# Output projection of a two-layer encoder by seven quadrant products, with weights summed by adding DMAs

## The chip, the cores and the metric

One core of a Trainium2 chip runs the whole program. The metric is device time per execution in microseconds (us); the median of repeated executions stands for a kernel.

The core has engines that run side by side, each with an in-order queue: PE (TensorE, matmuls), DVE (VectorE), ACT (ScalarE), POOL (GpSimd) and SP (SyncE, which here only issues DMAs). They wait for each other by semaphores. SBUF is the on-chip memory, PSUM the banks that matmuls write to.

## The reference

Two layers, 512 tokens, 1024 channels, all in float32. What matters here:

```python
def _mixer_sublayer(...):
    ...
    gates = jax.nn.sigmoid(gl + b_gate)
    ga, gb = jnp.split(gates, N_BRANCHES, axis=-1)
    return jnp.einsum('bsd,de->bse', ga * ya + gb * yb, w_out)

def reference(...):
    for i in range(DEPTH):
        h = _mixer_sublayer(...)
        x = _layer_norm(DEEPNORM_ALPHA * x + h, ln1_g[i], ln1_b[i])
        mlp = square(relu(x @ w_up[i])) @ w_down[i]
        gate = sigmoid(x @ w_ple_gate[i] + b_ple_gate[i])
        ple = gate * (p[i] @ w_ple[i])
        x = _layer_norm(DEEPNORM_ALPHA * x + mlp + ple, ln2_g[i], ln2_b[i])
```

`ya` and `yb` are the outputs of two kinds of attention, each with a projection of its own; `w_out` is the output projection that the change concerns, 512 x 1024 by 1024 x 1024 in each layer.

## The kernel before

**Products.** A float32 product is made of three matmuls: each operand is split into a high part, rounded to PE's format, and a low part, the rest; hi·hi, hi·lo and lo·hi are added in PSUM (`mm3`, `mm3t`). One matmul has 128 rows of depth and 512 columns of output.

**Weights.** They lie packed in DRAM (`wst`) in the order of use. `fetch` (L274) loads 128x1024 of them (512 KB) by SP into one of a few slots named `wst`; `prep` splits them. `split` (L248) takes the high part on ACT (a cast) and the low part on DVE (source minus high). `split_later` (L253) takes both on ACT, the low one as minus the high part, and POOL then issues an *adding DMA* that adds the source to it; which weights go that way is in the list `LATER`. High and low parts are tiles `whi`/`wlo` (three of each) or, for weights that stay longer, `bhi`/`blo`. A load is issued a few blocks ahead of use (`LOOK`), as soon as its slot is free.

**Order in a layer.** Attention; then for u = 0..3 the *second gates*: two gates (2u and 2u+1, of 128 channels each) as 24 matmuls each, tanh on ACT, then two `yb` products of 6 matmuls, a DVE step gate x `yb`, a POOL step that adds the first branch (`gate <- gate + ga`), and the split of the merged channels for the next product (`ahm` on ACT, `alm` on DVE). Then the output projection `wo`: 4 token tiles by 2 halves of 512 output channels by 8 depth blocks by 3 matmuls. DVE adds each result into the residual tile `y` (`projected`), takes its statistics (`moments`), and normalises (`normed`). PE transposes the normalised `y` (`turned`), and `embedding` (`ple`, from the input `p`, loaded as `pf` and split to `ph`/`pl`) and the embedding's gate (`embed`, `pg`) follow. Then comes the MLP, whose down projection already is made by seven products of quadrants in place of eight (class `Down`): both factors are cut into 2 x 2 blocks, seven products of sums of blocks are made, and each is added into or taken from one or more quadrants of the result. The weight sums are made on DVE there (`raw <- raw + raw`).

**What sets the order.** PE's order in these stages is that of the code (`manual_schedule`). A scheduler places the instructions of the other engines; within a queue each waits for those ahead of it. Pools (`np1`, `wb`, `rp`, ...) give tiles their memory, and a tile in memory that another used before waits for that one's last user.

Of the kernel before, what the change touches and what calls it, by code (L numbers as in the profile page):

```python
# [26 lines left out]
FQ = 4  # L27
UP_ORDER = (0, 4, 1, 5, 2, 6, 3, 7)
# [4 lines left out]
LATER = ((0, ("ple", 1, 0)), (1, ("start", 0)), *((l, n) for l in range(DEPTH) for n in (  # L33
# [27 lines left out]
def plan_layer(l):  # L61
# [31 lines left out]
    for u in range(4):  # L93
        out += [gate(1, 2 * u), gate(1, 2 * u + 1)]
        out.append((("bb", u), [("w_branch_b", l, [(i * P, P)], cols((t * P, P)))
                                for t in (2 * u, 2 * u + 1) for i in range(2)]))
# [5 lines left out]
    for h in range(2):  # L102
        out += k_outer(f"wo{h}", "w_out", blocks[4 * h:4 * h + 4])
# [17 lines left out]
def down_plan():  # L121

    return [((l, q, j, d, c), [("w_down", l, [((q * 8 + j * 4 + c * 2 + i) * P, P)], [(d * 512 + m * P, P)])
                               for i in range(2) for m in range(4)])
            for l in range(DEPTH) for q in range(FQ) for j in range(2) for d in range(2) for c in range(2)]
# [98 lines left out]
def build(nc, tc, plan, down, xw, xN, pT, wst, vec, rows, sink, cst, out):  # L224
# [3 lines left out]
    with ctx:  # L228
# [57 lines left out]
        def prep(c):  # L286
            st = fetched.pop(c)
            n = st.shape[-1]
            pool, tag, bufs = held_sets.get(plan[c][0][1][0], (wp, "w", 3))
# [37 lines left out]
        def linear(key, xs, ps=None):  # L327
            w = weights(key)
# [81 lines left out]
        def attention_block(l, av, rp, vt, OA, OB, begun):  # L410
            ct = rp.tile([P, cst.shape[1] - P], F32, tag="ct", name=f"ct{l}", bufs=1)
# [563 lines left out]
        def gate(l, b, t, vt, rp, ps=None):  # L975
            ps = linear((l, ("g", b, t)), X) if ps is None else ps
# [5 lines left out]
        class Tokens:  # L982


            def __init__(self, pool, y, name):
                self.pool, self.y, self.name, self.st, self.rs = pool, y, name, None, {}
# [19 lines left out]
            def steps(self, a, n=2, root=False, centre=True):  # L1006
# [8 lines left out]
                nc.vector.tensor_scalar(v, self.mv[:, a:a + n, 1], LN_EPS, None, ALU.add)  # L1015
# [71 lines left out]
        class Down:  # L1087
# [52 lines left out]
            def hidden(self, q, m, ps):  # L1140
# [16 lines left out]
                sr = self.qp.tile([P, 4, 256], F32, tag="sr", name=f"sr{self.l}_{q}_{kt}", bufs=1)  # L1157
# [14 lines left out]
            def half(self, q, n, s, c0=0, c1=512):  # L1172
# [3 lines left out]
                if first and not (s or c0):  # L1176
# [6 lines left out]
                for c in range(2):  # L1183
                    w = self.sets[n, c]
                    for i in range(2):
                        k, cols = 2 * c + i, slice(i * 512 + c0, i * 512 + c1)
                        for m, (a, b) in enumerate(((hi, 0), (hi, 1), (lo, 0))):
                            nc.tensor.matmul(ps, a[:, k, tok], w[b][:, cols], start=first and not (k or m),  # L1188
                                             stop=k == 3 and m == 2, skip_group_check=True)
# [16 lines left out]

        def pool(name, side="left"):
            c = ExitStack()
            return c.enter_context(tc.tile_pool(name=name, bufs=1, side=side, reuse_waits="tile")), c.close
# [6 lines left out]
        def embedding(l, h, PL, to, some=range(4)):  # L1216
            if 0 in some:
                ple["w"] = weights((0 if not h else l, ("ple", l, h)), 0)
            for a in some:
                ps = bank("mm", f"ple{l}_{h}_{a}")  # L1220
# [5 lines left out]
        for l in range(DEPTH):  # L1226
# [6 lines left out]
            oah, oal = (rp.tile([P, 4, S], F32R, name=f"oa{e}{l}", tag="oa" + e, bufs=1) for e in "hl")  # L1233
# [4 lines left out]
            ga = attention_block(l, av, rp, vt, OA, OB, begun)  # L1238
            av_close()

# [5 lines left out]
            np1, np1_close = pool(f"np{l}")  # L1246

            def pair(name):
                return (np1.tile([P, S], F32R, tag="ah", name="ah" + name, bufs=8),
                        np1.tile([P, S], F32R, tag="al", name="al" + name, bufs=8))  # L1250

            M = []
            for u in range(4):
                gs = [gate(l, 1, t, vt, np1) for t in (2 * u, 2 * u + 1)]
                w = weights((l, ("bb", u)))
                with in_turn(l):
                    nc.sync.dma_start(y[u], kept[u] if l else xN[u])
                if l and u:
                    add_row(y[u - 1], l - 1, 4)
                for n, g in enumerate(gs):  # L1260
                    t = 2 * u + n
# [8 lines left out]
                    M.append((mh, ml))  # L1270
            if l:
                add_row(y[3], l - 1, 4)
            rp_close()


            ph, pl = (np1.tile([P, 2, S], F32R, tag="p" + e, name=f"p{e}{l}", bufs=1) for e in "hl")
# [4 lines left out]
            split(ph, pl, pf)  # L1281
            PL = [(ph[:, k], pl[:, k]) for k in range(2)]
            wb, wb_close = pool(f"wb{l}", "right")
            held_sets.update({n: (wb, "b", 7) for n in ("wo1", "pg0", "pg1")})
            tn = Tokens(np1, y, f"n1_{l}")

            def projected(a, h, ps):
                x = y[a][:, h * 512:(h + 1) * 512]
                nc.vector.scalar_tensor_tensor(x, x, ALPHA, ps, ALU.mult, ALU.add)
                tn.moments(a, h)  # L1290
# [13 lines left out]
            def embed(a, h, ws):  # L1304
# [4 lines left out]
                t = np1.tile([P, S], F32, tag="tg", name=f"tg{l}_{h}_{a}", bufs=3)  # L1309
# [5 lines left out]
            with tc.manual_schedule(engines={PE}):  # L1315
                pss = [bank(t, f"wo{l}_0_{a}") for a, t in enumerate(("mm", "mm", "s", "s"))]
                for j in range(4):
                    w = weights((l, ("wo0", j)), 3)
                    for a in range(4):
                        for i in range(2):  # L1320
                            k = 2 * j + i
                            mm3t(pss[a], tokens(M[k], a), w, i, k == 0, k == KT - 1)
                for a in range(4):
                    projected(a, 0, pss[a])
                    if l:
                        ple[0, a] = np1.tile([P, S], F32, tag="ple0", name=f"ple{l}_0_{a}", bufs=4)
                        with in_turn(l):
                            nc.sync.dma_start(ple[0, a], kept_ple[a])
                ws = [weights((l, ("wo1", j)), 3 - j) for j in range(4)]
                for a in range(4):  # L1330
                    ahead(at[0] + a)
                    ps = bank("mm", f"wo{l}_1_{a}")
                    for k in range(KT):
                        mm3t(ps, tokens(M[k], a), ws[k // 2], k % 2, k == 0, k == KT - 1)
                    projected(a, 1, ps)
                    if a % 2:
                        normed(a - 1)
                turned(0)
                if not l:
                    embedding(l, 0, PL, np1)  # L1340
                else:
                    embedding(l, 1, PL, np1)
# [5 lines left out]
                if not l:  # L1348
                    turned(2)
                    embedding(l, 1, PL, np1)  # L1350
# [226 lines left out]
```

## Time and profile before

The median of 3 executions is 1504.73 us (1504.24 to 1506.15).

| | us |
|---|---|
| profiled execution, its own time | 1506.51 |
| its span in the profile | 1504.5 |
| attention and first part of layer 0 | 0 to 291.6 |
| last second gates, layer 0 | 291.6 to 318.8 |
| output projection `wo`, layer 0 | 318.8 to 362.4 |
| transposes, `ple` and `pg`, layer 0 | 362.4 to 420.3 |
| output projection, layer 1 | 1069.2 to 1112.7 |

By stage, each engine's busy time in the stretch (number of instructions), then PE's granted clock, the DMA engines' mean busy share, and GB/s:

```profile
291.60:318.80 27.20, 27.20 (x121) 22.53 (x121) 14.27 (x15) 10.33 (x14) 5.99 (x4) 1.00 0.35 107
318.80:362.40 43.60, 43.60 (x194) 36.04 (x194) 32.99 (x49) 17.98 (x18) 3.54 (x2) 1.00 0.48 148
362.40:420.30 57.90, 57.90 (x273) 48.49 (x272) 32.94 (x60) 21.73 (x38) 3.55 (x4) 1.00 0.58 180
```

The columns are PE, PEld (PE's weight load, which runs beside its matmuls), DVE, ACT and POOL. A busy PE is one that always has a matmul in its pipeline.

### The profile page before, as it was taken

How to read it: one execution, taken by the hardware profiler on the slowest of the kernel's cores; microseconds unless marked ns; L12 is line 12 of the kernel's file. 1: busy time of each engine (PE TensorE's matmuls, PEld its weight loads, DVE VectorE, ACT ScalarE, POOL GpSimd, SP SyncE). 2: the span in 40 equal slices, each digit the busy share in tenths (PEclk: the TensorE clock that was granted, in tenths of full speed). 3: DMA queues.
4: the chain of work that ended last, by engine and by line, in shares of the span. 5: the costliest groups of instructions: out<-in, count | busy, mean ns of one | idle time of the engine just before them, and what ended most of it. 6: DMA issues, size and time to landing. Idle time of an engine off the chain costs nothing.

```text
span 1504.5 us, 19451 instructions
## 1 busy us (share of the span) xinstructions
PE 1492.2 (99%) x7242; PEld 1241.7 (83%) x7242; DVE 1045.7 (70%) x1798; ACT 762.6 (51%) x1257; POOL 254.4 (17%) x216
## 2 busy tenths in 40 slices
PE   9999999999999999999999999999999999999997
PEld 7888888888888888888888888888888888888886
DVE  5766675458577777687877666754685877777778
ACT  4877764344344443434457777643442544444344
POOL 1212210110011110203012122102100202111121
PEclk9999999999999999999999999999999999999999
DMA  7656664555513415142366666555655233241403
GB/s 245 142 129 154 135 162 118 189 163 156 183 57 92 132 55 156 42 140 84 94 206 140 140 149 141 154 136 165 234 159 182 70 113 112 83 128 51 137 22 98
DMA packets 58174, 197.41 MB, mean 131 GB/s; under 512 B 7232, under 2 KB 7776, under 8 KB 58080
## 3 DMA queue, kind: packets, MB, share of 16 engines
q1 hardware_dynamic: 47120, 159.12, 32.9%
q0 software_dynamic: 10256, 36.70, 13.2%
q8 instruction: 56, 0.92, 0.3%
q10 hardware_dynamic: 704, 0.35, 0.1%
q14 instruction: 38, 0.31, 0.1%
HBM read 160.42 MB, written 6.37 MB: 111 GB/s over the span
## 4 chain that ended last, share of the span: by engine, by line
PE 93%; DVE 4%; ACT 2%; DMA 1%; issue 0%; POOL 0%; SPq 0%; DVEq 0%; POOLq 0%; ACTq 0%
PE dn L1188 19%; PE ps_up L316 8%; PE ps_up L315 8%; PE ps_up L314 8%; PE wo L322 2%; PE wo L321 2%; PE wo L320 2%; PE pg L320 2%; PE pg L322 2%; PE pg L321 2%; PE sa L541 1%; PE pta L504 1%; PE sb L536 1%; PE ps_start L315 1%; PE ps_start L314 1%; PE ya L314 1%
## 5 line engine op out<-in xcount | busy, mean ns | idle before, releaser
L250 ACT CAST whi<-wst 128x1024 fp32r<-128x1024 f32 (+1 forms) x115 | 117.7, 1024 | 248.2 <-PE ps_up L315 102.7
L251 DVE TENSOR_TENSOR wlo<-wst,whi 128x1024 fp32r<-128x1024 f32 (+1 forms) x115 | 144.1, 1257 | 98.9 <-ACT whi L250 97.8
L1151 POOL TENSOR_TENSOR hr<-r 128x512 f32<-128x512 f32 x64 | 108.9, 1702 | 547.3 <-ACT r L1143 516.0
L314 PE MATMUL ps_up<-xhi,whi 128*128 128x512 f32 x512 | 199.2, 389 | 0.0
L315 PE MATMUL ps_up<-xlo,whi 128*128 128x512 f32 x512 | 199.2, 389 | 0.0
L316 PE MATMUL ps_up<-xhi,wlo 128*128 128x512 f32 x512 | 199.2, 389 | 0.0
L315 PEld LDWEIGHTS ps_up<-xlo,whi 128*128 128x128 f32 x512 | 96.1, 188 | 20.0
L314 PEld LDWEIGHTS ps_up<-xhi,whi 128*128 128x128 f32 x512 | 96.1, 188 | 20.0
L316 PEld LDWEIGHTS ps_up<-xhi,wlo 128*128 128x128 f32 x512 | 96.1, 188 | 19.8
L1204 DVE TENSOR_TENSOR y<-y,dn 128x512 f32<-128x512 f32 (+1 forms) x98 | 65.8, 671 | 62.8 <-PE dn L1188 62.8
L250 ACT CAST whi<-raw 128x1024 fp32r<-128x1024 f32 x56 | 58.0, 1053 | 96.0 <-PE ps_up L315 57.6
L250 ACT CAST dhi<-raw 128x1024 fp32r<-128x1024 f32 x56 | 58.6, 1050 | 87.6 <-PE dn L1188 57.3
L257 POOL DMA_DIRECT2D wlo<-wst x54 | 47.5, 879 | 273.5 <-ACT wlo L256 188.8
L1131 DVE TENSOR_TENSOR raw<-raw,raw 128x1024 f32<-128x1024 f32 x64 | 84.6, 1322 | 0.3
L251 DVE TENSOR_TENSOR wlo<-raw,whi 128x1024 fp32r<-128x1024 f32 x56 | 68.3, 1219 | 14.1 <-ACT whi L250 14.1
L255 ACT CAST whi<-wst 128x1024 fp32r<-128x1024 f32 x54 | 56.6, 1048 | 30.2 <-PE ps_start L315 6.7
L251 DVE TENSOR_TENSOR dlo<-raw,dhi 128x1024 fp32r<-128x1024 f32 x56 | 68.8, 1238 | 3.6 <-ACT dhi L250 3.6
L256 ACT ACTIVATE wlo<-whi 128x1024 fp32r<-128x1024 f32 x54 | 57.3, 1061 | 0.9
L1188 PE MATMUL dn<-wlo,smh 128*128 128x512 f32 (+1 forms) x130 | 51.1, 393 | 0.2
L1162 DVE TENSOR_TENSOR sml<-sr,smh 128x1024 fp32r<-128x1024 f32 x32 | 43.7, 1365 | 10.8 <-ACT smh L1161 10.8
L1188 PE MATMUL dn<-whi,smh 128*128 128x512 f32 (+1 forms) x130 | 50.3, 390 | 0.0
L1188 PE MATMUL dn<-whi,sml 128*128 128x512 f32 (+1 forms) x130 | 50.3, 387 | 0.0
(867 smaller groups left out, 4044.1 us busy)
## 6 DMA issues: line engine op xcount, KB each, us to landing
wst<-wst SPq DMA_DIRECT2D x185, 512.0 KB, 3.6
raw<-wst SPq DMA_DIRECT2D x64, 512.0 KB, 4.4
wlo<-wst POOLq DMA_DIRECT2D x54, 512.0 KB, 4.9
y<-rows POOLq DMA_DIRECT2D x12, 512.0 KB, 6.5
row<-rows SPq DMA_DIRECT2D x7, 512.0 KB, 5.6
xs<-xw SPq DMA_DIRECT2D x6, 512.0 KB, 6.0
R<-line SPq DMA_DIRECT2D x24, 128.0 KB, 4.3
Ra<-linea SPq DMA_DIRECT2D x16, 128.0 KB, 3.5
```

Source lines behind the costliest of these rows:

```text
L250: nc.scalar.copy(hi, src)
L251: nc.vector.tensor_tensor(lo, src, hi.bitcast(F32), ALU.subtract)
L314: nc.tensor.matmul(ps, w[0][:, s], x[0], start=start, stop=False, skip_group_check=part)
L315: nc.tensor.matmul(ps, w[0][:, s], x[1], start=False, stop=False, skip_group_check=part)
L316: nc.tensor.matmul(ps, w[1][:, s], x[0], start=False, stop=stop, skip_group_check=part)
L320: nc.tensor.matmul(ps, x[0], w[0][:, c], start=start, stop=False)
L321: nc.tensor.matmul(ps, x[0], w[1][:, c], start=False, stop=False)
L322: nc.tensor.matmul(ps, x[1], w[0][:, c], start=False, stop=stop)
L1131: nc.vector.tensor_tensor(to, to, other, ALU.add)
L1151: nc.gpsimd.tensor_tensor(h.rearrange("p s t -> p (s t)"), r, r, ALU.mult)
L1188: nc.tensor.matmul(ps, a[:, k, tok], w[b][:, cols], start=first and not (k or m), stop=k == 3 and m == 2, skip_group_check=True)
L1204: return nc.vector.tensor_tensor(to, to, ps, ALU.subtract if n in (2, 4, 5) else ALU.add)
```

## The change

1. **Seven products for `wo`.** A class `Out(Down)` does the output projection by the scheme of the MLP's down projection. Channels c and c + 512 now make the two blocks of the depth, so the second gates go in pairs (u, u+4), and their merged channels are kept in a tile `hr` (four quadrants of 256 columns) from which the operands are taken: `a11`, `ax`, and sums `sr`, split to `smh`/`sml`. For u = 3 the gate's addition is on DVE, for the others on POOL as before.
2. **Weight sums by adding DMAs.** `w_out` is loaded by quadrant (`raw`, eight loads of 512 KB per layer), and the sums that the products need are made by eight adding DMAs per layer that read the weights from DRAM again. `cut` splits a product's weights (two tiles, `w..` for the first half of the depth and `d..` for the second; `whi0o4` is that of layer 0, product 4). For products 1 and 4 (`LATE`) the split is `split_later`.
3. **Result.** DVE adds each product, scaled, to `y` (`gather`), which is kept divided by ALPHA; the norm's epsilon is scaled to fit. Product 3 goes to three quadrants.
4. **More `split_later`:** `p`, `ple` and `pg0`'s first weights.
5. **Memory.** The pools are opened in another order: the tiles of `pf`, `bg` and `g1` now lie where the gates' tiles were, and `pg`'s weights where the seven products' tiles were.

```diff
+OUT = -1
+LATE = (1, 4)
...
-LATER = ((0, ("ple", 1, 0)), (1, ("start", 0)), *((l, n) for l in range(DEPTH) for n in (
+LATER = ((0, ("ple", 1, 0)), (0, ("ple", 0, 0)), (1, ("ple", 1, 1)), (0, ("pg0", 0)), (1, ("pg0", 0)), (1, ("start", 0)), *((l, n) for l in range(DEPTH) for n in (
...
+        class Out(Down):
+            SCALE = 0.5 / ALPHA
...
+            def load(self, j, d, c):
+                pool, tag, bufs = (wp, "wst", 3) if j else (self.qp, f"b{d}{c}", 1)
+                t = self.raw[j, d, c] = pool.tile([P, 1024], F32, name=f"raw{self.l}o{j}{d}{c}", tag=tag, bufs=bufs)
+                with in_turn(self.l):
+                    nc.sync.dma_start(t, self.rows_of(j, d, c))
+
+            def add(self, n, c):
+                to, other = {2: ((0, 0), (0, 1)), 3: ((0, 0), (1, 1)), 5: ((0, 1), (1, 1)), 6: ((0, 0), (1, 0))}[n]
+                nc.gpsimd.dma_start(self.raw[(*to, c)], self.rows_of(*other, c), accum_op=ALU.add)
+
+            def cut(self, n, c):
...
+                (split_later if n in LATE else split)(hi, lo, self.raw[j, d, c])
+                self.sets[n, c] = hi, lo
...
+            def gather(self, q, n, s, ps):
+                y, lo, up = self.y, slice(0, 512), slice(512, D)
+                lower = y[s + 2 * (n in (2, 5, 6))]
+                to = [(y[s][:, up], -1), (y[2 + s][:, up], -1), (y[2 + s][:, lo], 1)] if n == 3 else \
+                    [(lower[:, lo if n in (0, 1, 6) else up], -1 if n in (2, 4, 5) else 1)]
+                for t, sign in to:
+                    last = nc.vector.scalar_tensor_tensor(t, ps, sign * self.SCALE, t, ALU.mult, ALU.add)
...
             for u in range(4):
-                gs = [gate(l, 1, t, vt, np1) for t in (2 * u, 2 * u + 1)]
+                gs = [gate(l, 1, t, vt, mt, look=LOOK if u < 3 or t < 4 else 1) for t in (u, u + 4)]
...
-                    nc.gpsimd.tensor_tensor(g, g, ga[t], ALU.add)
-                    mh, ml = pair(f"m{l}_{t}")
-                    nc.scalar.activation(mh, g, AF.Copy, scale=0.5)
-                    nc.vector.scalar_tensor_tensor(ml, g, 0.5, mh.bitcast(F32), ALU.mult, ALU.subtract)
+                    h = hr[:, 2 - 2 * n:4 - 2 * n].rearrange("p s t -> p (s t)")
+                    (nc.vector if u == 3 else nc.gpsimd).tensor_tensor(h, g, ga[t], ALU.add)
+                    out7.mixed(hr, u, n, mt)
+                if u == 0:
+                    for c in range(2):
+                        out7.load(0, 0, c)
...
+                if u == 2:
+                    for c in range(2):
+                        out7.add(5, c)
+                        out7.cut(0, c)
+                        out7.add(2, c)
+                    for c in range(2):
+                        out7.load(1, 0, c)
...
-            split(ph, pl, pf)
+            split_later(ph, pl, pf)
...
-                for j in range(4):
-                    w = weights((l, ("wo0", j)), 3)
...
+                for n in range(7):
+                    if n < 2:
+                        for c in range(2):
+                            out7.cut(2 + n, c)
+                            out7.add((3, 6)[n], c)
+                            if not n:
+                                out7.load(1, 1, c)
+                    elif n < 5:
+                        for c in range(2):
+                            out7.cut(2 + n, c)
...
+                        for s in range(2):
+                            out7.gather(OUT, n, s, out7.half(OUT, n, s))
+                            behind(n, s)
```

**On PE**, where the output projection starts in layer 0 before (`wo0_0_0`: first half, first token tile):

```order
L320 MATMUL wo0_0_0_3245<-whi48_3165,ahm0_0_2915 128x512
L321 MATMUL wo0_0_0_3245<-wlo48_3166,ahm0_0_2915 128x512
L322 MATMUL wo0_0_0_3245<-whi48_3165,alm0_0_2916 128x512
L320 MATMUL wo0_0_0_3245<-whi48_3165,ahm0_1_2928 128x512
L321 MATMUL wo0_0_0_3245<-wlo48_3166,ahm0_1_2928 128x512
```

and product 4's first half after (`dn0_-1_2_0` is the PSUM bank, `smh`/`sml` the operand sums):

```order
L1191 MATMUL dn0_-1_2_0_3393<-whi0o4_3383,smh0_2845 128x512
L1191 MATMUL dn0_-1_2_0_3393<-wlo0o4_3384,smh0_2845 128x512
L1191 MATMUL dn0_-1_2_0_3393<-whi0o4_3383,sml0_2846 128x512
L1191 MATMUL dn0_-1_2_0_3393<-whi0o4_3383,smh0_2845 128x512
L1191 MATMUL dn0_-1_2_0_3393<-wlo0o4_3384,smh0_2845 128x512
```

The matmuls keep their shape, a product has 24 of them, and the second one of product 4 reads `wlo0o4`, the part that an adding DMA completes.

**On POOL**, from the last additions of the second gates of layer 0 to the norm's rows, before:

```order
L1266 TENSOR_TENSOR gate0_1_4_3062<-gate0_1_4_3062,gate0_0_4_2428 128x512
L1266 TENSOR_TENSOR gate0_1_5_3095<-gate0_1_5_3095,gate0_0_5_2542 128x512
L1266 TENSOR_TENSOR gate0_1_6_3161<-gate0_1_6_3161,gate0_0_6_2711 128x512
L1266 TENSOR_TENSOR gate0_1_7_3194<-gate0_1_7_3194,gate0_0_7_2785 128x512
L1084 DMA y0_0_2826<-rows 128x1024
```

and after (L1231 are weight sums, L259 low parts):

```order
L1319 TENSOR_TENSOR hr0o2_3134<-gate0_1_6_3125,gate0_0_6_2714 128x512
L1231 DMA raw0o000_2951<-wst 128x1024
L259 DMA wlo0o1_3290<-raw0o100_3175 128x1024
L1231 DMA raw0o000_2951<-wst 128x1024
L259 DMA pl0_3275<-pf0_3276 128x1024
L1231 DMA raw0o001_2953<-wst 128x1024
L1231 DMA raw0o000_2951<-wst 128x1024
L259 DMA dlo0o4_3389<-raw0o111_3311 128x1024
L259 DMA wlo0o4_3384<-raw0o110_3304 128x1024
L259 DMA wlo48_3517<-wst48_3514 128x1024
L259 DMA wlo49_3554<-wst49_3551 128x1024
L1086 DMA y0_0_2830<-rows 128x1024
```

Where POOL had nothing to issue between the last gate and the norm's rows, it now has ten adding DMAs; `wlo0o4` stands behind `pl0` and two sums of the first quadrant, `raw0o001` and `raw0o000`.

**On SP**, around the load of `pf`, before:

```order
L1257 DMA y0_3_2829<-xN 128x1024
L1279 DMA pf0_3232<-pT 128x1024
L1080 DMA row0_0_3234<-rows 128x1024
L1080 DMA row0_1_3236<-rows 128x1024
L283 DMA wst41_2932<-wst 128x512
```

and after:

```order
L285 DMA wst47_3179<-wst 128x512
L1227 DMA raw0o110_3304<-wst 128x1024
L1227 DMA raw0o111_3311<-wst 128x1024
L1344 DMA pf0_3276<-pT 128x1024
L1082 DMA row0_0_3278<-rows 128x1024
L1082 DMA row0_1_3280<-rows 128x1024
L285 DMA wst48_3514<-wst 128x1024
```

`pf0` and the two rows went out ahead of the weights of the second gates (`wst41`); now they go out behind all of these and the eight loads of `w_out`, and wait there for the last of the gates' tiles.

More of the change, by code (lines that the diff above doesn't have):

```diff
@@ L93, in plan_layer @@
     for u in range(4):
-        out += [gate(1, 2 * u), gate(1, 2 * u + 1)]
+        out += [gate(1, u), gate(1, u + 4)]
         out.append((("bb", u), [("w_branch_b", l, [(i * P, P)], cols((t * P, P)))
-                                for t in (2 * u, 2 * u + 1) for i in range(2)]))
+                                for t in (u, u + 4) for i in range(2)]))
     blocks = [cols((t * P, P)) for t in range(KT)]
@@ L1170, in product, with half @@
                 return last
-            def half(self, q, n, s, c0=0, c1=512):
+            def half(self, q, n, s, c0=0, c1=512, ks=range(4)):
                 name, _, tag, first = self.PRODUCTS[n]
                 hi, lo = self.op[name]
-                if first and not (s or c0):
+                if first and not (s or c0 or ks[0]):
                     self.bank = getattr(self, "bank", {})
@@ L1182, in half @@
                 tok = slice(s * P, (s + 1) * P)
[L1183 to L1189, printed above, removed]
+                for k in ks:
+                    w, i = self.sets[n, k // 2], k % 2
+                    cols = slice(i * 512 + c0, i * 512 + c1)
+                    for m, (a, b) in enumerate(((hi, 0), (hi, 1), (lo, 0))):
+                        nc.tensor.matmul(ps, a[:, k, tok], w[b][:, cols], start=first and not (k or m),
+                                         stop=k == 3 and m == 2, skip_group_check=True)
                 return ps
@@ L1214, in build, with embedding @@
         begun, ple = None, {}
-        def embedding(l, h, PL, to, some=range(4)):
+        def embedding(l, h, PL, to, some=range(4), tags=("mm",) * 4):
             if 0 in some:
@@ L1315, in build, with behind @@
             with tc.manual_schedule(engines={PE}):
-                pss = [bank(t, f"wo{l}_0_{a}") for a, t in enumerate(("mm", "mm", "s", "s"))]
-                for j in range(4):
-                    w = weights((l, ("wo0", j)), 3)
-                    for a in range(4):
[L1320 to L1326, printed above, removed]
+                def behind(n, s):
+                    if n == 1:
+                        tn.moments(s, 0)
+                    if n == 4:
+                        tn.moments(s, 1)
+                        if s:
+                            normed(0)
+                    if n == 5:
+                        tn.moments(2 + s, 1)
+                    if n == 6:
+                        tn.moments(2 + s, 0)
+                        if s:
+                            normed(2)
@@ L1327, in build @@
+                oq_close()
+                op_close()
+                np2, np2_close = pool(f"nq{l}")
+                held_sets.update({(l, (n, j)): (np2, "b", 8) for n in ("pg0", "pg1") for j in range(4)})
+                if l:
+                    for a in range(4):
+                        ple[0, a] = np2.tile([P, S], F32, tag="ple0", name=f"ple{l}_0_{a}", bufs=4)
                         with in_turn(l):
                             nc.sync.dma_start(ple[0, a], kept_ple[a])
-                ws = [weights((l, ("wo1", j)), 3 - j) for j in range(4)]
@@ L1330, in build @@
[L1330 to L1337, printed above, removed]
                 turned(0)
[L1339 to L1342, printed above, removed]
+                embedding(l, l, PL, np2, tags=("mm", "mm", "mm", "o"))
```

103 lines of the change are left out of this document (66 added, 37 removed).

## The prediction

> **What bounds the kernel now.** I read the page's busy shares first, then the chain of work that ended last.
>
> ```profile
> PE 1492.2 (99%) x7242; PEld 1241.7 (83%) x7242; DVE 1045.7 (70%) x1798; ACT 762.6 (51%) x1257; POOL 254.4 (17%) x216
> PE 93%; DVE 4%; ACT 2%; DMA 1%; issue 0%; POOL 0%; SPq 0%; DVEq 0%; POOLq 0%; ACTq 0%
> ```
>
> PE is busy 99% of the span and is 93% of the chain. Then I asked for every wait of PE, longest first, to see whether anything but matmuls costs time:
>
> ```profile
> PE out L1454 <- ACT y L1047: 1.5, 1, 1.5
> PE warm L244 <- DVE rgap L240: 1.0, 1, 1.0
> PE ps_start L314 <- ACT whi L402: 0.9, 1, 0.9
> ...
> PE xTn L1064 <- DVE y L1051: 0.6, 1, 0.6
> ```
>
> (total us, times, longest us). The longest wait is 1.5 us, at the very end. So a matmul taken out of the program is worth its whole place in the row, and a wait of PE that the change brings in costs its whole length. Every other engine counts only through such waits. These two rules make the sum.
>
> **What is removed.** The output projection, tile `wo`, in the windows that hold it in each layer, for its instructions alone:
>
> ```profile
> core 0: us, PE busy (x) PEld busy (x) DVE busy (x), PEclk, DMA share, GB/s
> 318.50:362.40 43.90, 43.56 (x192) 36.05 (x192) 4.66 (x7) 1.00 0.47 147
> 1068.50:1112.60 44.10, 43.44 (x192) 36.04 (x192) 4.74 (x7) 1.00 0.58 193
> ```
>
> 192 matmuls take 43.5 us in each layer, 0.2266 us apiece, at a granted clock of 1.00. Seven products of 24 matmuls make 168: 24 fewer in each layer, 48 x 0.2266 = **10.9 us** removed. The shape (128x512 output, 128 rows deep) stays, so the pace does too. The second gates are the same matmuls in another order: nothing.
>
> **What is added, and what hides it.** The durations that I use:
>
> ```profile
> L250 ACT CAST whi<-wst 128x1024 fp32r<-128x1024 f32 (+1 forms) x115 | 117.7, 1024 | 248.2 <-PE ps_up L315 102.7
> L251 DVE TENSOR_TENSOR wlo<-raw,whi 128x1024 fp32r<-128x1024 f32 x56 | 68.3, 1219 | 14.1 <-ACT whi L250 14.1
> L255 ACT CAST whi<-wst 128x1024 fp32r<-128x1024 f32 x54 | 56.6, 1048 | 30.2 <-PE ps_start L315 6.7
> L256 ACT ACTIVATE wlo<-whi 128x1024 fp32r<-128x1024 f32 x54 | 57.3, 1061 | 0.9
> L1162 DVE TENSOR_TENSOR sml<-sr,smh 128x1024 fp32r<-128x1024 f32 x32 | 43.7, 1365 | 10.8 <-ACT smh L1161 10.8
> L1289 DVE SCALAR_TENSOR_TENSOR y<-y,wo x16: 669/680/687, 340.0 to 1113.8; 128x512 f32<-128x512 f32 x16
> L995 DVE BATCH_NORM_STATS2 nstn<-y x8: 677/689/695, 342.3 to 364.9; 128x6 f32<-128x512 f32 x8
> ```
>
> DVE gathers 18 half-quadrants per layer instead of 8, at 0.68 us: 6.8 us more. Five of the seven products are split on DVE, 10 x 1.22 against 8 x 1.22 for `wo` before. The operand sums (`sr`, `sml`) of the last channel pair are some 3 us. The stage's room on DVE and ACT:
>
> ```profile
> core 0: us, PE busy (x) PEld busy (x) DVE busy (x) ACT busy (x) POOL busy (x), PEclk, DMA share, GB/s
> 318.50:340.30 21.80, 21.80 (x98) 18.06 (x97) 15.16 (x14) 10.79 (x12) 3.54 (x2) 1.00 0.66 210
> 340.30:362.40 22.10, 22.10 (x100) 18.23 (x99) 18.13 (x36) 7.19 (x7) 0.00 (x0) 1.00 0.29 84
> ```
>
> DVE was busy 33.3 us of 43.9. It will be nearly full in a stage of 38.1 us, with its queue in order. Followed row by row, the second token tile's normalised row comes about 0.9 us before PE wants to transpose it, if nothing earlier slips. I count it at nothing. If that cover were gone, each microsecond late would cost one. ACT has room: 18.0 of 43.9 us.
>
> **The adding DMAs.** They are the new resource, issued by POOL: eight weight sums per layer, and `ple`, `p`, `pg0`'s first and products 1 and 4 now take their low part by one, too. What the trace has of such transfers:
>
> ```profile
> L257 POOL DMA_DIRECT2D wlo<-wst x54: 853/877/1007, 26.4 to 995.4; - x54
> DMA to landing us min/median/max: 4.5/4.9/7.4
> q0 software_dynamic: 10256, 36.70, 13.2%
> ```
>
> An issue holds POOL for 0.88 us and the 512 KB land 4.9 us after its start. All adding DMAs (q0) moved 36.70 MB in 13.2% of the span's 1504.5 us: 185 GB/s, so 2.8 us with all 16 engines for each. The row-adding pair issued at 382.67 shows the same when two are in line:
>
> ```profile
> 382.67 1.76 POOL L1084 DMA_DIRECT2D y<-rows  x2 [16.30 <-PE xTn L1064]
> 384.20:386.90 2.70, 2.70 (x14) 2.22 (x13) 2.59 (x7) 2.31 (x6) 0.24 (x1) 1.00 1.05 197
> 386.90:389.60 2.70, 2.70 (x14) 2.23 (x13) 0.13 (x1) 1.77 (x3) 0.00 (x0) 1.00 1.01 190
> 389.60:391.00 1.40, 1.40 (x8) 1.17 (x7) 1.09 (x1) 0.00 (x0) 0.00 (x0) 1.00 0.07 15
> ```
>
> The DMA share stays at 1.0 for 5.4 us and then drops: they go one behind the other, 2.7 us each. So a queued one lands 2.7 us after the one ahead.
>
> The Trainium skill, "DMA: Bandwidth & Descriptors", section "Anatomy of one DMA — SWDGE (gpsimd) path", gives such a transfer 2.0 us plus its bytes at 436 GB/s; by that estimate one lands in 3.2 us, a queued one 1.2 us after another. The trace disagrees for the adding form: 4.5 us at the least, and 190 to 197 GB/s. By that figure of the Trainium skill the wait below would not exist, and the time would be that of rival A.
>
> **Where they fall late.** I follow the new order from the last second-gate matmul (layer 0; layer 1 has the same rows).
>
> ```profile
> 318.62 0.39 PE L316 MATMUL yb<-obh,wlo 128*128 128x512 f32 x1
> pf<-pT SPq DMA_DIRECT2D x3, 512.0 KB, 4.5
> wst<-wst SPq DMA_DIRECT2D x185, 512.0 KB, 3.6
> ```
>
> It ends at 319.0. Two DVE steps of 0.68 us make `hr0o3` at 320.4. Only then may `pf0`, which was loaded long before the gates until now, be fetched, since its tile takes the gates' memory. It lands at 324.9 by its own row (4.5 us). ACT, in order, casts `ph0` and `dhi0o3` and negates `pl0`: 328.1. POOL issues `pl0` (328.1) and one sum (329.0). Behind them stands the sum for product 6, which waits for DVE to be done with `wlo0o3`. ACT gets to `whi0o3` at 331.2; DVE has `sml`, two gathers and two statistics in between, and finishes `wlo0o3` at 333.8. So POOL issues that sum at 333.8, `dlo0o4` at 334.7 and `wlo0o4` at 335.6, though ACT's part of `dlo0o4` was done at 333.4. Landings: 328.1 + 4.9 = 333.0; + 2.7 = 335.7; 333.8 + 4.9 = 338.7; + 2.7 = 341.4; + 2.7 = 344.1. Product 4 begins four products (4 x 5.44) after 318.8, at 340.6, and its second matmul reads `wlo0o4` at 340.8. **PE waits 3.3 us.** Were `pf0` to land after 3.6 us, as plain weights do, it would wait 2.4.
>
> The bounds are farther out. Below: each adding DMA lands 4.9 us after its issue with no line, `wlo0o4` at 340.5, and the wait is 0. Above: the longest landing of the adding form, under load, is in this row:
>
> ```profile
> DMA to landing us min/median/max: 4.8/6.5/11.7
> ```
>
> 335.6 + 11.7 = 347.3, a wait of 6.5. I take **3.0 us** a layer, from the pair that was seen in line, nearest in kind; 6.0 in both. When PE stops there, everything behind it (DVE's statistics, the transposes) gains as much room, so no second wait follows from it.
>
> Smaller edits: `wlo0o1` is wanted about 0.9 us after it lands, and `wlo0o3` about 1 us after DVE writes it; the work of products 0 and 2 hides them, and I count nothing. The first raw weights of the MLP's down projection are now issued only when `pg` has read its last weights, as their tiles share memory with it. Six loads go ahead of the fourth up group's weights:
>
> ```profile
> q1 hardware_dynamic: 47120, 159.12, 32.9%
> raw<-wst SPq DMA_DIRECT2D x64, 512.0 KB, 4.4
> ```
>
> 159.12 MB in 32.9% of the span are 321 GB/s, 1.6 us a load. The sixth lands at 4.4 + 5 x 1.6 = 12.4 us, is split by 14.7, and is wanted after three groups of 24 matmuls, at 16.3. The three groups hide it; at worst 1 to 2 us a layer.
>
> **Sum.** The profiled execution took 1506.51 us, a span of 1504.5 and 2.0 outside it; the median shown is 1504.73. 1506.5 - 10.9 + 6.0 = 1501.6 for that execution, 4.9 less than it took; against the median, **1499.8 us**.
>
> **Rivals.** *A, no line.* The adding DMAs overlap with one another, or `pf0` lands early enough that they don't bunch. PE then never waits over about 1 us, and the time is 1504.7 - 10.9 = 1493.8, up to 1497. For it: isolated transfers land in 4.9 us, and the margin is then just met (340.5 against 340.8). Against it: the pair in line, 2.7 us each at full DMA share.
>
> *B, the adding DMAs are held up by plain loads (the other side).* After `pf0`, SP sends two 512 KB rows and the `ple` and `pg` weights into the same 16 engines while five adding DMAs are in line. If they then land like the slowest row, after 11.7 us, product 4 waits 6.5 us in each layer: 1504.7 - 10.9 + 13.0 = 1506.8, and more if `wlo0o1` at product 1 is late by as much. The point from which it decides is 5.44 us a layer: `wlo0o4` landing over 10.7 us after its issue. For it: DMA share was 0.66 already in this window. Against it: only one kind of row shows such a landing. The granted clock was 1.00 in all these windows and PE's longest wait 1.5 us, so what a longer wait does to the clock isn't in this trace. The Trainium skill, "TensorE: Matmul & The Clock Gate", section "What's actually happening", says that PE's clock halves after an idle window of about 3.4 us until it has been busy as long; by that, B would lose an estimated 1.7 us more per layer, some 1510 us.
>
> *C, thin margins.* DVE in its nearly full stage, `wlo0o1`, `wlo0o3` and the MLP's raw weights each are about 1 us from being late. Two of them late by 1 to 1.5 us in each layer, on top of the forecast, give 1502 to 1506: no change.
>
> **How the numbers follow.** A difference of 0.2%, 3.0 us, is about what a measurement of this kernel can tell from none, so faster means below 1501.7 and slower above 1507.7. Forecast (waits of 2 to 4 us a layer, 1498 to 1502): 0.45. A: 0.25. C: 0.19. B: 0.11, of which most lies above 1507. Faster: 0.25 and nearly all of 0.45, 0.67. Same: C and the edges of the others, 0.24. Slower: 0.09. The range goes from A's full gain, 1493.8, to B's price with product 4 alone, 1507.
>
> **What would show it.** In the profile after: 168 `dn` matmuls in each layer's output projection at 0.2266 us; in PE's waits one entry per layer of about 3 us, in which product 4's matmul waits for the landing of `wlo`; adding DMAs with a median landing well above 4.9 us; `pf` issued at about 320. No such wait and about 1494 would be A; a wait over 5 us, B; waits of `dn` or `xTn` on DVE or of `ps_up` on `whi`, C. The forecast is wrong above all if `pf0` isn't what sets the time of POOL's line, or if the line doesn't form.

## The result

The changed kernel takes 1520.55 us (median of 4, 1519.33 to 1524.04) against 1504.49 us for the kernel before: 1.0109 times as long, 95% interval 1.0090 to 1.0128. The forecast was 1499.8 us. The profiled execution took 1520.04 us, with a span of 1518.3 us: 13.8 us more than before.

From the page of the changed kernel, the busy shares, the two DMA queues, and the DMA issues of the weight sums (median us to landing):

```profile
PE 1488.2 (98%) x7194; PEld 1235.0 (81%) x7194; DVE 1073.0 (71%) x1854; ACT 792.3 (52%) x1291; POOL 272.7 (18%) x242
q1 hardware_dynamic: 47120, 159.12, 32.4%
q0 software_dynamic: 14576, 52.44, 18.7%
raw0o<-wst POOLq DMA_DIRECT2D x8, 512.0 KB, 8.5
raw1o<-wst POOLq DMA_DIRECT2D x8, 512.0 KB, 8.3
```

PE has its 48 matmuls less (7242 to 7194), and they are worth 10.9 us. Yet it is busy only 4.0 us less (1492.2 to 1488.2), and idle for 30.1 us of its span in place of 12.3. So the loss has two parts: 17.8 us more idle time, and 6.9 us in which PE is busy at a slower pace. -10.9 + 17.8 + 6.9 = 13.8. The adding DMAs moved 52.4 MB in place of 36.7, and a weight sum lands 8.5 us after its issue, where the low parts took 4.9 us in the trace of before.

PE's waits after (total us, times, longest):

```profile
PE dn_-1_2_0_3393 L1191 <- DMA wlo0o<-raw0o: 5.4, 1, 5.4
PE dn_-1_1_0_9875 L1191 <- DMA wlo1o<-raw1o: 4.3, 1, 4.3
PE dn_-1_2_0_9917 L1191 <- DMA wlo1o<-raw1o: 3.2, 1, 3.2
PE ps_start L318 <- DMA wlo<-wst: 1.7, 1, 1.7
PE out L1535 <- ACT y L1049: 1.5, 1, 1.5
PE pg L322 <- ACT ple L1275: 1.4, 1, 1.4
PE warm L246 <- DVE rgap L242: 1.0, 1, 1.0
PE dn_-1_0_0_9837 L1191 <- ACT a11h L252: 1.0, 1, 1.0
PE dn_-1_1_0_3351 L1191 <- DMA wlo0o<-raw0o: 0.9, 1, 0.9
...
PE dn_-1_0_0_9837 L1191 <- DVE a11l L253: 0.6, 1, 0.6
```

`dn_-1_2_0` is product 4, `dn_-1_1_0` product 1, and names ending in 9837 to 9917 are layer 1. Four of the waits are for low parts that an adding DMA completes: 5.4 and 0.9 us in layer 0, 4.3 and 3.2 in layer 1. Two others stand outside the projection: 1.7 us at the start of layer 1, 1.4 in `pg`.

The DMA engines over the projection. First before, then after (layer 0, layer 1):

```profile
core 0: us, PE busy (x) PEld busy (x) DVE busy (x) ACT busy (x) POOL busy (x), PEclk, DMA share, GB/s
318.80:346.00 27.20, 27.20 (x121) 22.53 (x121) 20.12 (x22) 12.62 (x13) 3.54 (x2) 1.00 0.68 212
1069.00:1108.00 39.00, 39.00 (x174) 32.30 (x173) 28.61 (x43) 14.73 (x15) 3.52 (x2) 1.00 0.64 216
```

```profile
318.80:346.00 27.20, 20.93 (x92) 16.47 (x90) 20.37 (x29) 13.51 (x15) 5.44 (x7) 0.94 1.03 233
1069.00:1108.00 39.00, 29.99 (x122) 23.36 (x120) 24.69 (x35) 19.36 (x22) 7.07 (x8) 0.95 0.99 235
```

They are full from end to end (1.03 and 0.99, where 0.68 and 0.64 stood), and the granted clock is below 1.00. The DMA records give the landings, here for layer 0 (us from the span's start):

```
issued   landed   took   what
319.21   325.02    5.8   pf
319.59   327.65    8.1   row bg
320.53   332.56   12.0   row g1
320.67   332.37   11.7   sum for product 3
323.79   333.54    9.8   weights of ple
328.45   335.89    7.4   pl (low part of p)
329.07   338.38    9.3   sum for product 6
335.10   340.86    5.8   sum for product 6
336.20   343.37    7.2   dlo of product 4
338.68   345.84    7.2   wlo of product 4
```

And POOL's timeline there (start, us, idle time before and its releaser):

```profile
328.45 0.88 POOL L259 DMA_DIRECT2D pl<-pf  x1 [6.90 <-ACT pl L258]
329.07 1.15 POOL L1231 DMA_DIRECT2D raw0o<-wst  x1
335.10 0.86 POOL L1231 DMA_DIRECT2D raw0o<-wst  x1 [4.88 <-DVE wlo0o L253]
336.20 0.87 POOL L259 DMA_DIRECT2D dlo0o<-raw0o  x1 [0.23 <-issue]
338.68 0.87 POOL L259 DMA_DIRECT2D wlo0o<-raw0o  x1 [1.61 <-ACT dhi0o L252]
```

The sum for product 3 took 11.7 us beside `pf`, two rows and the next weights. ACT stood for it and cast `whi0o3` at 332.4, DVE was done with the low part at 334.7, and POOL went on at 335.1:

```profile
332.39 1.05 ACT L252 CAST whi0o<-raw0o 128x1024 fp32r<-128x1024 f32 x1 [2.01 <-DMA raw0o<-wst]
```

The last two issues come 0.3 us after the landings of `pl` (335.89) and of the first sum for product 6 (338.38). For the second of them the profile names ACT, but its part of that `wlo` had been done since 336.3. PE then resumes slowly. Its timeline at the end of the wait, and the three stretches behind the long waits:

```profile
345.89 0.80 PE L1191 MATMUL dn_-1_2_0_3393<-wlo0o,smh 128*128 128x512 f32 x1 [5.38 <-DMA wlo0o<-raw0o]
346.48 0.63 PE L1191 MATMUL dn_-1_2_0_3393<-whi0o,sml 128*128 128x512 f32 x1
346.91 0.63 PE L1191 MATMUL dn_-1_2_0_3393<-whi0o,smh 128*128 128x512 f32 x1
```

```profile
345.90:349.40 3.50, 3.50 (x8) 2.81 (x9) 0.29 (x1) 0.00 (x0) 0.00 (x0) 0.50 0.56 200
1086.70:1090.10 3.40, 3.40 (x8) 2.68 (x9) 0.48 (x1) 2.50 (x3) 0.00 (x0) 0.51 1.04 307
1108.10:1114.00 5.90, 5.90 (x14) 4.64 (x15) 1.26 (x3) 0.00 (x0) 0.00 (x0) 0.50 0.43 133
```

Matmuls start 0.43 us apart, not 0.227, at a granted clock of 0.50. 12.8 us pass so, and half of them, 6.4 us, are lost. That is nearly all of the 6.9 us found above.

### The profile page after: what moved, and what is told of

It is laid out like the page before. It is cut to its first block, busy times and chain, and to the rows that moved or that the text cites. A ratio compares the mean times of both kernels' runs of the same rounds, so it can differ in the third digit from the quotient of the medians.

```text
span 1518.3 us, 19532 instructions
## 1 busy us (share of the span) xinstructions
PE 1488.2 (98%) x7194; PEld 1235.0 (81%) x7194; DVE 1073.0 (71%) x1854; ACT 792.3 (52%) x1291; POOL 272.7 (18%) x242
## 5 line engine op out<-in xcount | busy, mean ns | idle before, releaser
L252 ACT CAST whi<-wst 128x1024 fp32r<-128x1024 f32 (+1 forms) x105 | 107.2, 1021 | 214.8 <-PE ps_up L317 102.7
L253 DVE TENSOR_TENSOR wlo<-wst,whi 128x1024 fp32r<-128x1024 f32 (+1 forms) x105 | 131.4, 1257 | 63.3 <-ACT whi L252 62.6
L259 POOL DMA_DIRECT2D wlo<-wst x58 | 50.9, 878 | 315.8 <-ACT wlo L258 216.6
L257 ACT CAST whi<-wst 128x1024 fp32r<-128x1024 f32 x58 | 60.8, 1048 | 47.3 <-PE dn_-1_2_1_9918 L1191 9.4
L258 ACT ACTIVATE wlo<-whi 128x1024 fp32r<-128x1024 f32 x58 | 61.5, 1061 | 1.1
```

The source lines that it names most:

```text
L252: nc.scalar.copy(hi, src)
L253: nc.vector.tensor_tensor(lo, src, hi.bitcast(F32), ALU.subtract)
L257: nc.scalar.copy(hi, src)
L258: nc.scalar.activation(lo, hi.bitcast(F32), AF.Copy, scale=-1.0)
L259: nc.gpsimd.dma_start(lo, src, accum_op=ALU.add)
```

## The experiments

Theory **Q**: the adding DMAs, in line on full DMA engines, are what PE waits for. Rival **F**: the late load of `pf` holds ACT's in-order queue, and that sets everything behind it. Theory **K**: the clock's half pace after the waits is a cost of its own. Each kernel below is the changed kernel with the edit shown; times are medians. The kernel before was measured beside each of them on the same chip and took 1503.9 to 1504.5 us, so the chips differ by under 1 us.

**late_none**: products 1 and 4 split on DVE.

```diff
-LATE = (1, 4)
+LATE = ()
```

> Products 1 and 4 take their low part on DVE, not by an adding DMA (LATE empty): four adding DMAs fewer per layer, 4 x 1.22 us more on DVE. Theory Q (the queue of adding DMAs on full DMA engines is what PE waits for): the waits on wlo of products 1 and 4 (0.9 + 5.4 in layer 0, 4.3 + 3.2 in layer 1) go, and with them the half clock behind them (6.5 us); about 1520.5 - 13.8 - 6.5 = 1500 us, up to 1506 if DVE, now fuller, is late elsewhere. Rival F (the late load of pf blocks ACT's queue, and that sets everything behind it): ACT is still held until 325 (layer 0) and 1087 (layer 1), so products 2 to 4 wait as long for their splits: 1510 to 1516 us.

1506.36 us against 1504.20, ratio 1.0012 (1.0003 to 1.0022). Its longest waits, and the DMA share in the projection:

```profile
PE pg L322 <- ACT ple L1275: 1.9, 1, 1.9
PE dn_-1_2_1_3390 L1191 <- DVE y L1254: 1.9, 1, 1.9
PE dn_-1_2_1_9910 L1191 <- DVE y L1254: 1.8, 1, 1.8
PE ps_start L318 <- DMA wlo<-wst: 1.7, 1, 1.7
PE ps_('g', 1, 3)_9703 L316 <- DVE gate L1317: 1.6, 1, 1.6
```

```profile
318.80:346.00 27.20, 25.29 (x112) 20.63 (x111) 23.86 (x34) 12.34 (x15) 3.51 (x4) 1.00 0.77 191
1069.00:1108.00 39.00, 36.66 (x160) 29.39 (x159) 32.96 (x57) 20.66 (x23) 4.39 (x5) 1.00 0.72 174
```

No wait of the projection on a landing is left among its longest, the clock is 1.00, and 14.2 us of the loss are gone, as Q says. What is left are waits of under 2 us: for DVE and ACT, and the one at the start of layer 1. They eat the gain.

**nosums**: no weight sums.

```diff
             def add(self, n, c):
...
-                nc.gpsimd.dma_start(self.raw[(*to, c)], self.rows_of(*other, c), accum_op=ALU.add)
+                return
```

> Leaves out the eight weight sums per layer (products 2, 3, 5 and 6 use single quadrants), so the time of the sums' adding DMAs is taken away with nothing put in their place; all matmuls, splits and loads stay. Theory Q: the DMA share in the output projection falls to about 0.7, every wait of dn on a landing is below 1 us, no half clock: 1496 to 1499 us. Rival F: pf still lands at about 325 and 1085 behind its late issue, ACT's chain stays, product 4 waits 2 to 3 us in each layer: 1503 to 1508 us.

1502.63 us, ratio 0.9988 (0.9978 to 0.9997). The DMA share is 0.74 in layer 0:

```profile
318.80:346.00 27.20, 27.20 (x120) 22.26 (x120) 22.80 (x37) 15.43 (x16) 3.44 (x4) 1.00 0.74 188
```

Layer 0 has no wait there, though `pf` is as late (issued at 318.1) and product 4 has its adding DMAs: against F. In layer 1 product 1 still waits 2.3 us: its part took 7.8 us to land beside a row addition issued 3.2 us ahead of it, where layer 0's took 5.4. So the sums cost some 18 us, more than the 10.9 that the matmuls give; this run takes away their transfers, POOL's time for them and the splits' waits for them all at once. Even without them the change is worth only 1.6 us.

**warm**: extra matmuls where PE waited.

```diff
+                        for i in range({(0, 4): 24, (1, 1): 19, (1, 4): 14}.get((l, n), 0)):
+                            idle = bank("o", f"idle{l}_{n}") if not i else idle
+                            x = out7.op[out7.PRODUCTS[n][0]][0]
+                            nc.tensor.matmul(idle, x[:, i % 2, :P], out7.sets[n, 0][0][:, :512], start=True, stop=True)
```

> PE gets 24, 19 and 14 extra matmuls into an unused PSUM bank ahead of product 4 of layer 0, product 1 and product 4 of layer 1, as long as its waits there (5.4, 4.3, 3.2 us), on operands that are there; nothing else changes. Theory K (after these waits PE runs at half clock for 3.6, 3.4 and 6.0 us, which costs 6.5 us in all): the granted clock stays at 1.00 and the time falls by about 6.5, to 1514 us. Rival (the half clock lies inside the waits and costs nothing, or it comes anyway): 1520 us.

1516.89 us, 3.7 less than the changed kernel. The stretch that held the first long wait (the columns are those of the windows above):

```profile
340.00:350.00 10.00, 9.95 (x45) 7.86 (x44) 5.76 (x8) 2.01 (x3) 0.00 (x0) 1.00 0.79 195
```

The clock stays at 1.00 to the end of the stage, so it was the waits that halved it. 3.7 of the 6.4 us come back. Of the rest, 1.2 us went into a new wait of product 4 in layer 1 for DVE; where the other 1.5 went isn't settled.

**rowsheld** and **held2**: the rows later.

```diff
-                bg, g1 = row(np1, l, 0, "bg"), row(np1, l, 1, "g1")
+            bg, g1 = (np1.tile([P, D], F32, tag=t, name=f"row{l}_{i}", bufs=1) for i, t in enumerate(("bg", "g1")))
...
+                        if n == 3:
+                            for i, r in ((1, g1), (0, bg)):
+                                nc.vector.tensor_scalar(r[:, 0:2], y[2 + i][:, 0:2], -1.0, None, ALU.mult)
+                                with in_turn(l):
+                                    nc.sync.dma_start(r, rows[l, i].partition_broadcast(P))
```

> The two row loads (bg, g1) behind pf wait until product 2 is added, so they leave the stretch in which the sum for product 3 is made. Theory Q: that sum, issued at 320.7 and landing 11.7 us later, lands some 3 us sooner, and so do the ones behind it; product 4 of layer 0 waits 2 to 3 us in place of 5.4, product 1 of layer 1 (whose part is ahead of the rows) 3 to 4 in place of 4.3; about 1515 us. Rival F: ACT is held by pf alone, 1519 to 1521 us.

1520.34 us, the same. The edit missed its aim: product 2 doesn't write the columns that it reads, and in the trace (of an execution of 1516.2 us) the rows went out at 322.8 and 323.3, only some 3 us later than in the changed kernel. `held2` reads `y[2 + i][:, 512:514]`, which product 2 does write.

> The edit of rowsheld read columns that product 2 does not write, so the rows were late by 2.4 us only; here they wait for product 2 in fact (issued at about 336 in place of 319.6). pf, LATE and LATER stay as in the changed kernel. If the rows' 2 x 512 KB on the same 16 DMA engines are what makes the sum for product 3 land 11.7 us after its issue, it now lands after 6 to 8 us; product 4 of layer 0 waits 1 to 3 us (5.4 in the changed kernel), product 1 of layer 1 under 3 (4.3): 1510 to 1514 us. If the rows don't matter, 1518 to 1521 us.

1521.29 us, the same again. Now the rows were issued at 334.4 and 341.2, and the sum for product 3 landed 8.8 us after its issue in place of 11.7. But the rows now met product 4's parts: its `dlo` took 10.0 us, and PE waited 4.0 us for it. In layer 1 product 4 no longer waited, but `pg` did, for 3.7 us: ACT had stood 4.5 us for a late load of weights. So it isn't these loads alone; there is too much to move in the stretch, and what is moved out of one transfer's way gets into another's.

**earlypf**: `pf` in memory of its own, loaded ahead of the gates. To make room, the second gates' tiles are two deep in place of three.

```diff
-            g = rp.tile([P, S], F32, tag=f"gate{b}", name=f"gate{l}_{b}_{t}", bufs=3 if b else 8)
+            g = rp.tile([P, S], F32, tag=f"gate{b}", name=f"gate{l}_{b}_{t}", bufs=2 if b else 8)
...
+            np0, np0_close = pool(f"n0{l}")
+            pf = np0.tile([P, 2, S], F32, tag="pf", name=f"pf{l}", bufs=1)
+            with in_turn(l):
+                nc.sync.dma_start(pf, pT[l])
             op, op_close = pool(f"op{l}")
```

> pf gets memory of its own beside the gates (gate tiles two deep in place of three) and is loaded ahead of them; the split of p, its adding DMA and all else stay. Rival F (pf's late landing holds ACT's queue, and that sets the rest): ACT is free at 320 in place of 325 (layer 0) and 1080 in place of 1088 (layer 1), product 4 waits under 2 us, 1511 to 1513 us. Theory Q (the adding DMAs in line on full DMA engines): 512 KB less in the crowded stretch, so each later landing comes some 1.5 us sooner, but the line stays, and product 1 of layer 1 waits on: 1515 to 1518 us.

1515.21 us, 5.3 less. Its two longest waits:

```profile
PE dn_-1_1_0_3354 L1191 <- DMA wlo0o<-raw0o: 4.0, 1, 4.0
PE dn_-1_1_0_9882 L1191 <- DMA wlo1o<-raw1o: 3.6, 1, 3.6
```

Product 4 waits in neither layer now, but for two reasons. In layer 1 its `wlo` landed at 1100.4 in place of 1108.0, ahead of PE. It was issued 4.2 us sooner, as ACT no longer stood 7.5 us for `pf`, and took 3.5 us less to land: F and Q each have a part there. In layer 0 its lateness isn't shown to come from `pf`: its two parts landed at 344.1 and 346.6 (345.8 and 343.4 in the changed kernel), no sooner on the whole, and PE only came to product 4 at 345.7 in place of 340.1. What held PE up was product 1, which now waits 4.0 us: the rows went out at 318.1 and 318.5 (319.6 and 320.5 before this edit), beside its `wlo`, which landed after 8.7 us in place of 5.6. For the whole, the time is the one that Q gave.

**none_pf, none_pf_later, none_pf_later_tags**: no late parts and `pf` early; then also the added `LATER` entries out; then the `ple` banks as before.

> LATE empty (as late_none) and pf loaded ahead of the gates (as earlypf). In late_none PE waited 1.9 and 1.8 us for DVE's addition of product 1, which stood behind a split that ACT could begin only when pf had landed. If that is so, both waits go: 1506.4 - 3.7 = 1502.7 us. If DVE itself is full (4 x 1.22 us more on it per layer), the waits stay or move: 1505 to 1507 us.

1506.91 us (1.0021, 1.0012 to 1.0031): as late_none. One wait for DVE's addition fell to 0.2, the other stayed at 1.6, and one of 1.2 us for a gate's tanh on ACT is new; whether the shorter row of gate tiles makes it wasn't tried.

```diff
-LATER = ((0, ("ple", 1, 0)), (0, ("ple", 0, 0)), (1, ("ple", 1, 1)), (0, ("pg0", 0)), (1, ("pg0", 0)), (1, ("start", 0)), *((l, n) for l in range(DEPTH) for n in (
+LATER = ((0, ("ple", 1, 0)), (1, ("start", 0)), *((l, n) for l in range(DEPTH) for n in (
```

> As none_pf, and the entries that the change added to LATER are taken out (ple of each layer and pg0's first are split on DVE as before): two adding DMAs fewer per layer, one or two DVE steps more at the transposes. Theory Q predicts no loss from fewer adding DMAs; if DVE is what is full behind product 6, PE waits for the transposes' or pg's operands by 1 to 2 us per layer, 1503 to 1506; if not, as none_pf or 1 us less.

1515.43 us, 8.5 more for two fewer adding DMAs per layer. The first of its waits:

```profile
PE xTn L1066 <- DVE y L1053: 7.9, 7, 4.3
```

The transposes wait 7.9 us in all, up to 4.3 at once, for DVE's normalised rows, which stand behind splits in its queue. The timelines of DVE and ACT ahead of the longest of these waits, in layer 1:

```profile
1128.69 1.23 DVE L253 TENSOR_TENSOR blo<-wst,bhi 128x1024 fp32r<-128x1024 f32 x1 [3.57 <-ACT bhi L252]
1127.61 1.05 ACT L252 CAST bhi<-wst 128x1024 fp32r<-128x1024 f32 x1 [3.39 <-DMA wst<-wst]
```

DVE wasn't full there: it stood 3.6 us for a split whose weights took 8.7 us to land, beside two row additions. Two of the shorter waits, in layer 0, do lie where DVE is nearly full (18.8 us busy of the 20 from 352 on), but it is as busy there in none_pf (19.0 us), which has none of them. So what stands ahead of a step in DVE's queue seems to matter more than how full DVE is.

> As none_pf_later, and the second ple of layer 0 takes its four PSUM banks from the three of tag mm as before the change, which forces ACT's copies out of them earlier. The wait of pg on ACT's copy of ple (1.4 to 1.9 us in all runs of the change, none before) should go: 1.5 us less than none_pf_later. If ACT's order and not the banks makes it, no change, or PE waits inside ple instead.

1518.90 us, 3.5 more. The wait of `pg` on ACT's copy is gone, but one of 1.4 us inside `ple` is there in its place, which fits ACT's order and not the banks. What makes the time longer isn't settled.

**pf_held, pf_held_4, pf_held_none**: `pf` early with rowsheld's edit, and LATE of (1, 4), (4,) and none.

> Both moves at once: pf loaded ahead of the gates (earlypf) and the rows held until product 2 is added (rowsheld); the adding DMAs of products 1 and 4 stay. If the two loads together are what pushed the line past its margin in layer 0, products 1 and 4 there wait under 1 us each (5.4 and 0.9 in the changed kernel, 4.0 at product 1 in earlypf). In layer 1 three row additions stand in POOL's line ahead of product 1's part, which neither move touches, so it still waits 3 to 4 us and loses some 2 to 3 us to the half clock: 1508 to 1511 us. If the waits are the sums' alone, as large as in earlypf: 1514 to 1516.

> As pf_held, and product 1 is split on DVE, so two adding DMAs per layer leave the line just where it fails in layer 1; product 4 keeps its adding DMAs, which spare DVE 2.4 us per layer against none_pf. If the line and DVE each have just room for this share: no wait on a landing over 1 us, no half clock, 1502 to 1504 us, level with the kernel before or a little better. If DVE is short anyway, 1505 to 1507 as none_pf.

> As none_pf with the rows held as well. No adding DMA for a low part stands in the projection, so PE there waits for DVE alone, and holding two loads changes little: 1505.5 to 1507 us, within 1.5 us of none_pf. If DMA traffic still set its waits, 2 to 3 us less.

1511.03, 1512.63 and 1513.93 us. The rows were hardly held, as told. In pf_held product 4 of layer 0 still waited 3.4 us and product 1 of layer 1 2.9. The other two came out some 6 and 7 us above the highest time expected: there the scheduler put DVE's split of product 3's sum ahead of the addition of product 1. DVE's timeline of pf_held_none:

```profile
330.18 1.23 DVE L253 TENSOR_TENSOR wlo0o<-raw0o,whi0o 128x1024 fp32r<-128x1024 f32 x1 [4.59 <-ACT whi0o L252]
331.32 0.68 DVE L1254 SCALAR_TENSOR_TENSOR y<-dn_-1_1_0_3350,y 128x512 f32<-128x512 f32 x1
```

DVE stood 4.6 us for a sum that landed at 329.1, with the addition of product 1 behind it, and PE waited 3.6 us for that. A late landing on one in-order engine turns into a wait that names another. With the rows truly held (same order on DVE):

> none_pf with the rows truly held. In pf_held_none the scheduler set DVE's split of product 3's sum ahead of the addition of product 1, and PE waited 3.6 and 4.1 us for that; the same order stands here. With the rows held the sum lands at about 326 in place of 329 and the wait falls to about 1 us per layer: 1504 to 1508 us, against 1513.9. If it doesn't fall, the rows aren't what delays the sum.

1506.94 us, 7.0 less: the sum landed after 5.5 us in place of 7.8, and these waits fell to 1.3 and 1.6 us. Here, with `pf` early and four adding DMAs fewer per layer than in held2, the rows do matter.

**none_held2, none_held2_ct**: LATE empty, rows truly held, `pf` as in the changed kernel; then also the constants of layer 1 held.

> LATE empty and the rows truly held; pf as in the changed kernel. In late_none PE waited 1.9 and 1.8 us for DVE, which stood behind the split of product 3's sum, landed late. With the rows out of the way the sum lands 3 us sooner, both waits go: 1506.4 - 3.7 = 1502.7 us. If DVE's own load makes them, 1505.5 to 1507 us.

1504.60 us, ratio 0.9997 (0.9988 to 1.0005): level with the kernel before. The two waits for DVE are gone: the sum for product 3 landed after 6.0 us in layer 0 (8.8 in late_none), so it was the late sum and not DVE's own load that made them.

```diff
+                if l:
+                    nc.vector.tensor_scalar(ct[:, 0:2], X[7][0][:, S - 2:].bitcast(F32), -1.0, None, ALU.mult)
                 with behind_x(not l):
                     nc.sync.dma_start(ct, cst[:, :off])
```

> As none_held2, and in layer 1 the load of the constants (ct, 960 KB), which the new pools let go out at 750 us in place of 757, waits for the last transposed columns of layer 0. PE's wait at the start of layer 1 for an adding DMA that lands 10.6 us after its issue (1.6 to 1.8 us in every run of the change, none before) should go: 1.7 us less than none_held2, about 1501 us. If ct isn't what it collides with, no change.

1502.56 us against 1504.13, ratio 0.9986 (0.9978 to 0.9994): the only version with all its work that beats the kernel before, by 1.6 us. The wait at the start of layer 1 is gone: the constants went out at 766.1, and the adding DMA that they had met landed after 6.5 us, not 10.6. Its longest wait:

```profile
PE pg L322 <- ACT ple L1277: 2.2, 1, 2.2
```

## Why the prediction was wrong

**The matmuls removed (10.9 us): right.** In late_none, where the clock stays at 1.00, PE is busy 1482.1 us, 10.1 less than before.

**The wait of product 4 (3.0 us per layer): right in kind, too small, and in layer 0 set by another link.** It was 5.4 and 3.2 us, 8.6 in place of 6.0. POOL's line did form, behind DVE's `wlo0o3` as worked out. But what held `wlo0o3` in layer 0 wasn't ACT's work after `pf`: ACT stood 2.0 us for the sum for product 3, which was taken to be in time and took 11.7 us. (In layer 1 ACT did stand for `pf`, 7.5 us.) The last issue came at 338.7, not 335.6, as POOL, it seems, also stood for landings; its landing came at 345.8, not 344.1.

**"`wlo0o1` is wanted about 0.9 us after it lands ... I count nothing": this step failed.** Product 1 waited 0.9 us in layer 0 and 4.3 in layer 1, 5.2 us where nothing was counted. "layer 1 has the same rows" was wrong for POOL, which has row additions there:

```profile
1073.73 0.87 POOL L1086 DMA_DIRECT2D y<-rows  x1 [6.06 <-DMA y<-kept]
1075.40 0.86 POOL L259 DMA_DIRECT2D wlo1o<-raw1o  x1 [0.80 <-ACT wlo1o L258]
```

It wasn't the issue of product 1's part that was late: it came 0.4 us after ACT was done, and 6.5 us ahead of product 1, where layer 0 had 4.4. The landing was: 11.2 us, beside the row addition, `pf` and more, against 5.6 in layer 0. The DMA share of 0.66, quoted for rival B, should have been added up with the 2.7 us of all 16 engines that each adding DMA takes. Measured, it came to 1.03 and 0.99, and at that share no margin of about 1 us holds.

**"A wait of PE that the change brings in costs its whole length": it costs more.** Half clock behind three waits added 6.4 us. The Trainium skill, "TensorE: Matmul & The Clock Gate", section "What's actually happening", was cited for this, in rival B alone; the runs bear its direction out. Its window of about 3.4 us of idleness is longer than what was needed here: the clock halved 2.1 us (layer 0, product 4) and 2.4 us (layer 1, product 4) after PE had stopped.

**DVE "nearly full": the sum wasn't made.** The terms given (33.3 us, and 6.8, 2.4 and 3 more) come to 45.5 us, which doesn't fit into 38.1; what leaves DVE is not listed. Measured, DVE was busy 34.9 of 39.6 us in layer 0 of late_none (318.5 to 358.1).

**Terms not foreseen.** 1.6 us for product 0's operands in layer 1, 1.7 at the start of layer 1 (the constants, shown by none_held2_ct), 1.4 in `pg`. All together: -10.9 + 8.6 + 5.2 + 6.4 + 1.6 + 1.7 + 1.4 = 14.0, against 13.8 in the spans.

**The rivals.** B came true in kind: landings of 11.7 us beside plain loads and a full set of DMA engines, at a chance of 0.11. Its price by rows, 1506.8, left out product 1 and the halved clock. A's condition, no line, holds in layer 0 of nosums, where the sums are left out. C's small waits are what remains in late_none and none_held2.

**The rate by the Trainium skill.** The Trainium skill, "DMA: Bandwidth & Descriptors", section "Anatomy of one DMA — SWDGE (gpsimd) path", would have an adding DMA land in an estimated 3.2 us. The 16 sums here took 8.5 us in the middle, 5.6 at the least. On this the trace of before was the better guide, and was not followed far enough.

## What to carry to other kernels

A saving of matmuls is worth its time only if what feeds them has room: add up the DMA share, DVE's work and each in-order line over the stage, not one transfer at its median. A wait that names an engine can be a late landing one or two links back: follow it through the engine's idle time before moving work. Here the change came out level only with four adding DMAs per layer taken out and the loads that could wait moved away. A wait of PE of about two microseconds or more should be priced with the halved clock behind it.

## What the runs showed of the hardware that was not expected

**Three adding DMAs at a time.** In the 17 traces, 138 adding DMAs were issued while two others were under way, and none while three were. Of these, 20 were issued 0.31 us after a landing, as the last two of layer 0 above: POOL seems to stand until one of three has landed. That the limit is one of number, not of bytes, wasn't tried.

**The clock is judged step by step, not wait by wait.** A wait of 2.3 us (nosums, layer 1) was followed by 3.4 us at half clock, and in pf_held one of 1.9 us, the half clock beginning 1.4 us after PE had resumed. In late_none two waits of 1.9 us were not followed by any. All these stretches are 3.41 us or twice that, and in each of the 17 traces every change of the granted clock lies on one fixed grid of 3.413 us (after the change the stretches begin at 342.64, 1086.75 and 1107.23, which are 218 and 6 steps apart). PE's idle time, added up in each step of this grid up to 1480 us (short of the kernel's end), sorts them: of the steps at full clock, all 21 with 1.8 us of it or more were followed by a step at half clock, none with less than 1.7, and two of the six between. In late_none no step has more than 1.67 us. So, as far as these traces go, a wait costs more than its length when more than about half of a step is idle, and then up to 1.7 us for each step at half clock; a wait of under 3.4 us can fall either way by where it lies. This may be part of why late_none's times spread over 5.3 us, where the kernel's before, measured beside it, spread over 3.3.
